# Moving the output stores of a multiply-and-GELU kernel to the ScalarE queue, in four pieces, each issued when its columns are done

## The chip, the cores and the metric

One core of a Trainium2 chip runs the kernel. The metric is the device time in microseconds (us), reported as the median of several runs. All runs quoted here were classed as fast (none is over 1.5% above the fastest run of its kernel), the profiled ones at a granted TensorE clock of 1.0, which is full speed. The span of a profile runs from the first instruction to the last and is some 1.3 us shorter than the reported time.

## The reference

```python
x, y: 1024 x 4096 float32
z = x * y
out = 0.5 * z * (1 + tanh(sqrt(2 / pi) * (z + 0.044715 * z ** 3)))
```

Two arrays of 16.78 MB are read and one is written. There is one multiply (VectorE) and one GELU (ScalarE) for each element.

## The kernel before

The arrays are seen as 128 partitions by 32768 columns. All of x has its own place in SBUF (the core's on-chip memory), where the product and the GELU are written too. Of y only 16384 columns fit at a time, so its second half is loaded in two quarters, each when the multiplies have freed its place. Everything that moves data is issued from SyncE, in this order: x first half, y first half, x second half, y third quarter, y last quarter, store of the first half, store of the second half.

```python
X_LOADS = [(0, 16384), (16384, 32768)]
Y_LOADS = [(0, 16384, 0), (16384, 24576, 0), (24576, 32768, 8192)]
STEP = 4096
STORES = [(0, 16384), (16384, 32768)]
...
    load_x(1)
    for i in (1, 2):
        nc.sync.wait_ge(sem_mul, (Y_LOADS[i][1] - Y_LOADS[1][0]) // STEP)
        load_y(i)
...
        nc.vector.wait_ge(sem_y[i], 16)
        for c in range(a, b, STEP):
            nc.vector.tensor_mul(...).then_inc(sem_mul, 1)
            n += 1
            nc.scalar.wait_ge(sem_mul, n)
            nc.scalar.activation(..., func=GELU).then_inc(sem_act, 1)

    for i, (a, b) in enumerate(STORES):
        nc.sync.wait_ge(sem_act, b // STEP)
        nc.sync.dma_start(out=out_r[:, a:b], in_=xs[:, a:b]).then_inc(sem_o[i], 16)
```

## Time and profile before

| before | |
|---|---|
| time | 120.78 us (120.68 to 120.92) |
| span of the profile | 119.5 us |
| DMA engines busy | 98.5% of the span |
| VectorE, ScalarE busy | 29%, 25% |
| last load lands | 80.79 us |
| last GELU ends | 93.30 us |

In the profile, "DMA" is the mean of the core's 16 DMA engines; its row cuts the span into 40 slices and gives tenths of busy time. "L87 DVE" is the multiply and "L94 ACT" the GELU. "SPq" and "ACTq" are issues of transfers on SyncE's and ScalarE's queues: one takes about 0.34 us and says nothing of how long the data move. (A line marked x2 spans from the start of its first issue to the end of its last.) The time of the data is in "to landing", the time from the issue to the last byte's completion. The lines themselves stand in the prediction below.

### The profile page before, as it was taken

The numbers are of one execution on the slowest core, as the hardware profiler recorded it, in microseconds if no ns is written. First come the engines' busy times: TensorE is split into PE (matmuls) and PEld (weight loads), VectorE is DVE, ScalarE is ACT, GpSimd is POOL, SyncE is SP. The second block draws the span as 40 slices with busy tenths as digits, with TensorE's granted clock in tenths as the row PEclk, the third lists the DMA queues.
The fourth block names the chain that finished last, engine by engine and source line by source line (L and its number), as shares of the span: only waits on it lengthen the run. The fifth ranks groups of instructions, "written<-read, shape, count | busy, mean of one in ns | idle before, by whom it ended". The sixth has DMA issues, their size and how long they took to land.

```text
span 119.5 us, 68 instructions
## 1 busy us (share of the span) xinstructions
DVE 35.0 (29%) x8; ACT 30.2 (25%) x9; POOL 0.2 (0%) x4
## 2 busy tenths in 40 slices
DVE  0000000000000199999600049959990000000000
ACT  3000000000000006797780000977479200000000
POOL 0000000000000000000000000000000000000000
DMA  9889888998899889988898989998899888988890
GB/s 351 351 373 680 351 351 351 636 417 351 351 636 417 351 351 526 526 351 351 351 526 351 504 373 482 395 526 351 351 395 658 351 351 351 702 351 351 351 680 22
DMA packets 1008, 50.33 MB, mean 421 GB/s; under 512 B 112, under 2 KB 112, under 8 KB 112
## 3 DMA queue, kind: packets, MB, share of 16 engines
q1 hardware_dynamic: 1008, 50.33, 98.5%
HBM read 33.55 MB, written 16.78 MB: 421 GB/s over the span
## 4 chain that ended last, share of the span: by engine, by line
DMA 53%; DVE 22%; ACT 3%; SPq 0%; issue 0%; DVEq 0%
DMA ys<-in_y_dram 53%; DVE xs L87 22%; ACT xs L94 3%; SPq L66 0%; DVEq L85 0%
## 5 line engine op out<-in xcount | busy, mean ns | idle before, releaser
L87 DVE TENSOR_TENSOR xs<-xs,ys 128x4096 f32<-128x4096 f32 x8 | 35.0, 4421 | 54.7 <-DMA ys<-in_y_dram 54.7
L94 ACT ACTIVATE xs<-xs 128x4096 f32<-128x4096 f32 x8 | 28.9, 3617 | 61.1 <-DVE xs L87 61.1
L94 ACT ACT_TABLE_LOAD x1 | 1.3, 1283 | 1.9 <-PEq L54 1.9
L120 POOL MEMSET const-bfloat16-1.0<- 128x1 bf16 x1 | 0.1, 102 | 0.0
L120 POOL MEMSET const-uint8-127<- 128x1 uint8 x1 | 0.1, 102 | 0.0
L120 POOL MEMSET const-float32-1.0<- 128x1 f32 x1 | 0.1, 99 | 0.0
L120 POOL MEMSET const-float32-0.0<- 128x1 f32 x1 | 0.1, 98 | 0.2 <-issue 0.2
## 6 DMA issues: line engine op xcount, KB each, us to landing
ys<-in_y_dram SPq DMA_DIRECT2D x2, 4096.0 KB, 21.1
xs<-in_x_dram SPq DMA_DIRECT2D x2, 40.3
out_dram<-xs SPq DMA_DIRECT2D x2, 31.9
ys<-in_y_dram SPq DMA_DIRECT2D x1, 40.8
```

The source lines that it names most:

```text
L87: nc.vector.tensor_mul(out=xs[:, c : c + STEP], in0=xs[:, c : c + STEP], in1=ys[:, r + c - a : r + c - a + STEP],).then_inc(sem_mul, 1)
L94: nc.scalar.activation(out=xs[:, c : c + STEP], in_=xs[:, c : c + STEP], func=GELU).then_inc(sem_act, 1)
L120: nc = _bacc.Bacc("TRN2", target_bir_lowering=False, num_devices=1)
```

## The change

The intent is to send out results as soon as they exist, on a queue of their own, so that they need not stand behind all loads.

```diff
-STORES = [(0, 16384), (16384, 32768)]
+STORES = [(0, 8192), (8192, 16384), (16384, 24576), (24576, 32768)]
...
             ).then_inc(sem_act, 1)
+            for k, (sa, sb) in enumerate(STORES):
+                if sb == c + STEP:
+                    nc.scalar.wait_ge(sem_act, n)
+                    nc.scalar.dma_start(
+                        out=out_r[:, sa:sb], in_=xs[:, sa:sb]
+                    ).then_inc(sem_o[k], 16)
 
-    for i, (a, b) in enumerate(STORES):
-        nc.sync.wait_ge(sem_act, b // STEP)
-        nc.sync.dma_start(out=out_r[:, a:b], in_=xs[:, a:b]).then_inc(sem_o[i], 16)
```

The text calls the four stores A to D, as the prediction does.

## The prediction

> **What bounds the kernel now.** I began with the page: its table of slices and its queue table say whether the engines that compute or the transfers set the time.
>
> ```profile
> span 119.5 us, 68 instructions
> DVE 35.0 (29%) x8; ACT 30.2 (25%) x9; POOL 0.2 (0%) x4
> ...
> DVE  0000000000000199999600049959990000000000
> ACT  3000000000000006797780000977479200000000
> ...
> DMA  9889888998899889988898989998899888988890
> ...
> q1 hardware_dynamic: 1008, 50.33, 98.5%
> ```
>
> VectorE and ScalarE stand idle for two thirds of the span. The 16 DMA engines are busy in every slice to the end, 98.5% of the span in all, on one queue. Every byte moved is needed (two inputs and one output of 16.78 MB), so the kernel is bound by transfers with hardly a gap, and the change removes no byte. It can only close or open gaps.
>
> The next view is the chain that ended last, in order of time, to see when each load lands, then the order of all instructions, to see when each store could go.
>
> ```profile
> 0.44 40.80 DMA ys<-in_y_dram
> ...
> 58.80 21.99 DMA ys<-in_y_dram
> ...
> 80.88 8.77 DVE xs L87 x2
> ...
> 89.68 3.62 ACT xs L94
> ```
>
> ```profile
> 50.13 3.62 ACT L94 ACTIVATE xs<-xs 128x4096 f32<-128x4096 f32 x1 [0.72 <-DVE xs L87]
> ...
> 58.80 3.62 ACT L94 ACTIVATE xs<-xs 128x4096 f32<-128x4096 f32 x1 [0.72 <-DVE xs L87]
> 62.45 31.22 SPq L100 DMA_DIRECT2D out_dram<-xs  x2
> ```
>
> The last load (y of the last 8192 columns) lands at 58.80 + 21.99 = 80.79 us; two multiplies and one GELU later, at 93.30, everything is computed. This last 12.5 us of arithmetic costs nothing, because the first store, 8.39 MB, was issued at 62.45 and stands in the same queue right behind the loads. The view of the store line shows how long it stood there:
>
> ```profile
> L100 SPq DMA_DIRECT2D out_dram<-xs x2: 343/346/348, 62.4 to 93.3; - x2
> ...
> DMA to landing us min/median/max: 26.1/31.9/37.7
> ```
>
> It lands at 62.45 + 37.7 = 100.1, that is 19.4 us after the last load: the 17.6 us before that it only waited its turn. The second store is issued at 93.3, before the first has ended, and lands at 93.3 + 26.1 = 119.4. So **the first store is a stock of 19.4 us of transfers that is kept back until the loads are over and covers the 12.5 us of arithmetic behind the last load.** That is what I look at in the change.
>
> The unit of a transfer is in the trace's records of single packets: one row of 64 KB takes 2.418 us on its engine and one of 32 KB 1.213 us, loads and stores alike; each engine carries 8 of the 128 rows. 16 x 65536 B / 2.418 us is 434 GB/s. So a transfer of 16384 columns takes 8 x 2.418 = 19.3 us and one of 8192 columns 8 x 1.213 = 9.7 us.
>
> **What the Trainium skill says.** (1) "DMA: Bandwidth & Descriptors", section "Where 436 GB/s comes from", gives 435 GB/s as the ceiling of the 16 engines; the 434 GB/s above agrees, so no faster rate is to be had from a second queue. (2) The same page, "Issuing engines are not separate DMA queues": transfers issued from ScalarE and SyncE run on the same 16 engines and interleave, and a second issuer saves only issue time. The kernel before has one queue, so its trace can't show this. (3) The same page, "Queues, rings and completion order": each engine goes round-robin between the queues that have work, a packet at a time. This is the step my number rests on most; again nothing in the trace before shows it, and the trace after will. (4) "Perfetto Trace Analysis", section "DMA Optimizations", recommends one issuing engine for inputs and another for outputs, and smaller chunks that start sooner, the latter where the DMA engines are generally idle. Here they are not: 98.5%.
>
> **The change part by part.** *Removed:* SyncE's two store issues and their waits for GELU; off the path until the end. *Added on ScalarE:* four waits for its own GELUs and four issues. An issue took 0.346 us on SyncE; I take the same, and 0.1 us (a guess) for the wait. ScalarE has 0.72 us of idle time before each GELU (the brackets above), so 0.45 us fits in, and the GELUs before the last pair are not late. *Moved:* where the stores lie among the loads. I name the four stores A to D and work through the time.
>
> The first packet of x moves 1.0 us after its issue starts in the packet records. A is ready at 50.13 + 3.62 = 53.75; with 0.1 for the wait and 1.0 to the first packet it moves from 54.8. B is ready at 62.42 and can move from 63.5. From 54.8 on both queues have work. The loads alone would have ended at 80.8. With equal turns, x's second half (5.8 us left, 2.4 packets of 64 KB) gives way to 2.4 packets of A: 2.9 us, landing near 63. Then come the 8 packets of y's third quarter against 8 of A and B: 9.7 + 9.7 = 19.4 us, landing at 82 to 83 in place of 70.3. Then y's last quarter: 8 packets against the 5.6 that A and B have left. By then all of A and B, 2 x 9.7 = 19.4 us, has gone ahead of the last load: 80.8 + 19.4 = 100.2. How turns are shared hardly matters to this sum, as long as the stores get about half.
>
> C is ready when y's third quarter, landed at 82.5, is through: two multiplies (8.76), a GELU (3.62) and 0.15 of waits, 95.0; it moves from 96, when some 2 to 3 packets of the last load are left, and takes 1 or 2 turns, 1.2 to 2.4 us. I worked through the turns of one engine packet by packet with these durations: the last load lands at 101.5, A and B are done by 95.5, C by 108.8. That working lands the old loads at 79.7, 1.1 us before their 80.8, because the records show a few packets of 1.8 to 3.2 us and some skew between engines; I take half of it as carried over: 102.0.
>
> Then the end, with nothing left to cover it: 102.0 + 0.1 (start) + 8.76 (two multiplies) + 3.62 (GELU) = 114.5. Meanwhile C has ended near 109.3 and the engines stand idle. D: 0.1 for the wait, 1.0 to the first packet, 8 x 1.213 = 9.7, and 0.3 from the last packet to the landing (records: 119.07 against 119.4): 11.1 us. The sum is 125.6 us of span. The profiled run before was reported at 120.85 us for a span of 119.5, so 1.35 more: **about 126.9 us**. As a check by gaps: the engines stand idle from 109.3 to about 115.6, 6.3 us, and 120.8 + 6.3 = 127.1. The gain of D being half as long as the old second store is nothing, since only the total and the gaps count.
>
> **The rivals.** *Loads keep precedence* (the stores get few turns while loads are queued): then A and B wait as before, the last load lands near 81, A to D drain behind it without a gap, and the time is 120.5 to 121. For it: the loads were issued long before. Against it: the skill's round-robin. A half-way share would land the last load early and leave some stock, 121 to 125. *Traffic in both directions at once moves more than 434 GB/s*: if a load and a store overlapped fully, the last load would land near 82, computing ends at 94.5 and D lands at 105.6, about 107 us. Against it: a load and a store cost the same 2.418 us a packet in the records and the skill has one ceiling for the engines. *Mixing costs rate*[...]: 3% over the some 45 us of mixing would add 1.3 us, for 128.3. No mixed stretch exists in the trace before, so I can't size it. *ScalarE becomes the bound* because its queue also issues: 25% busy, 0.72 us of slack a turn; if each issue took 1 us it would add 0.7 us at the end only.
>
> **Range and chances.** The fair-share sum gives 125 to 128 with the packet at which C comes in, the skew and the issue cost varied; the mixing loss would stretch it to 129, an uneven share would pull it down. I say 126.7, and 124.2 to 128.6 for eight times in ten. Slower by over 2% means above 123.2: 0.86, the fair share with any of its sizes. Within 2% needs load precedence or nearly: 0.10. Faster needs overlap of both directions: 0.04.
>
> **What would show the steps right or wrong.** Right: the wait of VectorE before y's third quarter grows from 11.7 to some 24 us and the last load lands near 102; the stores from ScalarE's queue land 20 us or more after issue for A and B and some 11 for D; the DMA row has a gap of 5 to 7 us near 109 to 115 and is full again to the end; the chain that ended last now ends with a store of about 11 us behind GELU; multiplies still take 4.42 and GELUs 3.62 us. Wrong: a last load at 81 (precedence), more than 440 GB/s while both queues are busy (overlap), packets longer than the shares explain (mixing loss), or GELUs that start late behind an issue (ScalarE).

## The result, and the profile after

The changed kernel takes **126.7 us** (126.5 to 126.73), against 120.81 us for the kernel before in the same rounds. The ratio is 1.0484, with a 95% interval of 1.0466 to 1.0502. A ratio is the mean time of one kernel's fast runs over that of the other's of the same rounds, so it is not quite the ratio of the medians. The change makes the kernel 4.8% slower.

The page of the changed kernel, its head, its table of slices and its queues:

```profile
span 125.4 us, 71 instructions
...
DVE 35.0 (28%) x8; ACT 30.2 (24%) x9; POOL 0.2 (0%) x4
...
DVE  0000000000000799997000000039940059920000
ACT  3000000000000037977900000000976001974000
...
DMA  9799799789779979999699999999999999703977
...
q1 hardware_dynamic: 720, 33.55, 63.1%
q10 hardware_dynamic: 576, 16.78, 31.0%
```

VectorE is busy for the same 35.0 us and ScalarE for the same 30.2. What is new is the second queue, q10, and a hole in the DMA row in the slices just before the last four, while VectorE and ScalarE work by themselves. In the packet records no engine moves anything from 109.72 to 115.00 us: **5.28 us**. The span grew by 5.9. The packets of both queues together took 118.0 us of an engine's time, against 117.7 before, so 0.3 us more is busy time, and the rest of the growth is idle.

The chain that ended last, in order of time (start, us, what):

```profile
0.42 40.92 DMA ys<-in_y_dram
...
58.90 42.72 DMA ys<-in_y_dram
...
101.71 8.77 DVE xs L87 x2
...
110.51 3.62 ACT xs L94
```

The last load is issued at 58.90, as before, but lands after 42.72 us and not after 21.99: at 101.62 instead of 80.79. The two multiplies and the GELU behind it take as long as ever. The order of instructions shows what went ahead of it:

```profile
53.88 0.38 ACTq L100 DMA_DIRECT2D out_dram<-xs  x1
...
62.55 0.34 ACTq L100 DMA_DIRECT2D out_dram<-xs  x1
83.55 8.76 DVE L87 TENSOR_TENSOR xs<-xs,ys 128x4096 f32<-128x4096 f32 x2 [24.68 <-DMA ys<-in_y_dram]
...
95.99 0.34 ACTq L100 DMA_DIRECT2D out_dram<-xs  x1
...
114.15 0.34 ACTq L100 DMA_DIRECT2D out_dram<-xs  x1
```

These are the four stores. A and B are issued 48 and 39 us before the last load lands, and are gone by then: B's last packet ends at 97.1. VectorE's wait for y's third quarter (in brackets) has grown from 11.70 to 24.68 us. The view of the store line gives the landings:

```profile
L100 ACTq DMA_DIRECT2D out_dram<-xs x4: 338/339/375, 53.9 to 114.2; - x4
...
DMA to landing us min/median/max: 11.1/19.7/36.1
```

D, issued last, needs 11.1 us to land and has the engines to itself. Finally the windows view of two stretches (VectorE, ScalarE and POOL busy, clock, DMA share, GB/s):

```profile
64.00:95.00 31.00, 8.76 (x2) 6.27 (x2) 0.00 (x0) 1.00 1.01 436
110.00:115.00 5.00, 0.47 (x1) 3.62 (x1) 0.00 (x0) 1.00 0.02 7
```

While loads and stores take turns, the engines carry 436 GB/s, as much as one queue of loads alone (435 in the first 41 us of the kernel before; the ends of such a window cut packets, so a few per cent are not to be read). The packet records are sharper: every one of the 395 rows of 32 KB that lie wholly within 64 to 95 us, 195 of loads and 200 of stores, took 1.213 us, the median of such a row on one queue. In the five microseconds before D the engines carry next to nothing.

### The profile page after: what moved, and what is told of

It reads as the page before. It is cut to its first block, busy times and chain, and to the rows that moved or that the text cites. A ratio compares the mean times of both kernels' runs of the same rounds, so it can differ in the third digit from the quotient of the medians.

```text
span 125.4 us, 71 instructions
## 1 busy us (share of the span) xinstructions
DVE 35.0 (28%) x8; ACT 30.2 (24%) x9; POOL 0.2 (0%) x4
## 4 chain that ended last, share of the span: by engine, by line
DMA 67%; DVE 21%; ACT 3%; SPq 0%; issue 0%; DVEq 0%
DMA ys<-in_y_dram 67%; DVE xs L87 21%; ACT xs L94 3%; SPq L66 0%; DVEq L85 0%
```

## The experiments

My theory: A and B were a stock of transfers that covered the arithmetic behind the last load, and the change spends it too early. The rivals are that ScalarE's queue costs something by itself, that smaller stores do, or that loads and stores in the same stretch slow each other. The first four kernels take the change apart, and of the last four, e7 is a half dose and the others try to bring the time back by other ways than undoing it. All gave correct results. For a whole view first (the hole is the time in which the packet records show no data packet on any engine; "before" took 120.95 us in both groups of runs, and 120.81 in the rounds of the change; landing and hole are of the one profiled execution, which in e2 was its slowest, 135.76 us):

| kernel | last load lands | hole before the last store | time | ratio to before |
|---|---|---|---|---|
| before | 80.79 | none | 120.95 | 1 |
| split alone (e1) | 80.89 | none | 120.99 | 1.0005 |
| move alone (e2) | 101.05 | 13.67 | 135.14 | 1.1166 |
| change, A and B held (e3) | 86.63 | none | 121.42 | 1.0034 |
| one queue, A and B first (e4) | 100.60 | 3.96 | 125.49 | 1.0371 |
| change, pieces of 4096 (e5) | 91.73 | none | 121.15 | 1.0014 |
| change, pieces of 2048 (e6) | 86.19 | none | 121.34 | 1.0038 |
| change, B held (e7) | 96.51 | 0.43 | 121.74 | 1.0064 |
| change, finer last quarter (e8) | 101.41 | none | 121.06 | 1.0010 |
| the change | 101.62 | 5.28 | 126.70 | 1.0484 |

In every row the time is that of before in the same rounds, plus the hole, plus 0.0 to 0.6 us.

### e1: the split alone

```diff
 # the kernel before, with
-STORES = [(0, 16384), (16384, 32768)]
+STORES = [(0, 8192), (8192, 16384), (16384, 24576), (24576, 32768)]
```

> The split alone: four stores of 8192 columns, all on SyncE's queue behind the loads, as in the kernel before. Theory (the stock of early stores is spent before the last load, so the arithmetic after it is bare): here nothing goes ahead of the last load, it lands at 80.8 us as before, and the time is that of before, 120.5 to 121.3. Rival (stores of 8192 columns, that is rows of 32 KB and twice as many packets, cost by themselves): 123 or more.

It took 120.99 us, ratio 1.0005 (0.9987 to 1.0023). The last load in the chain lands at 80.89:

```profile
58.61 22.28 DMA ys<-in_y_dram
```

Four stores with rows of 32 KB cost nothing against two with rows of 64 KB. That rival falls.

### e2: the move alone

```diff
 # the changed kernel, with
-STORES = [(0, 8192), (8192, 16384), (16384, 24576), (24576, 32768)]
+STORES = [(0, 16384), (16384, 32768)]
```

> The move alone: the two stores of 16384 columns go on ScalarE's queue as soon as their columns are done, without the split. Theory: the first store, 64 KB packets taking turns with 32 KB load packets, is all gone before the last load lands near 99 to 101; then 12.5 us of arithmetic with no transfer at all, then a store of 19.4 us: 133 to 136, worse than the change as a whole. Rival (the second queue or the issue on ScalarE costs a fixed amount per store): two issues instead of four, so 124 or less.

It took 135.14 us, ratio 1.1166 (1.1144 to 1.1189), by far the slowest, with half as many issues on ScalarE as the change. So no fixed cost per store can be the cause. Its DMA row shows the whole of the last arithmetic bare:

```profile
DMA  9997979979789797799998999899940000979777
```

The hole is 13.67 us long. The split, which costs nothing in e1, is thus worth 8.4 us once the stores go early: in the change, C is still there to cover part of the arithmetic.

### e3: the change with A and B held until y's third quarter has landed

```diff
 # the changed kernel, with (shortened: the kernel keeps 0 and 1 in a tuple)
+            if n == 5:
+                nc.scalar.wait_ge(sem_y[1], 16)
+                for k in (0, 1):
+                    store(k, 4)   # the wait on sem_act and the issue, as in the change
             nc.scalar.wait_ge(sem_mul, n)
...
-                if sb == c + STEP:
+                if sb == c + STEP and k not in (0, 1):
```

> The changed kernel, but ScalarE holds its first two stores until y's third quarter has landed (70.3 us), so that they share with the last load only. Queue, split, issues and mixing stay. Theory: the last load lands at 88 to 92 in place of 101.6, the second store and the third are the stock behind it, no gap, and the time is that of before, 120.5 to 121.5. Rivals (ScalarE's queue, the size of stores, loss by mixing loads and stores): 123.5 to 127.

It took 121.42 us, ratio 1.0034 (1.001 to 1.0058). ScalarE still issues all four stores, and A still takes turns with a load. The instructions in order of time, A and B issued together, the last quarter's multiplies, and the DMA row:

```profile
70.16 0.86 ACTq L84 DMA_DIRECT2D out_dram<-xs  x2
...
86.73 8.76 DVE L95 TENSOR_TENSOR xs<-xs,ys 128x4096 f32<-128x4096 f32 x2 [7.74 <-DMA ys<-in_y_dram]
```

```profile
DMA  9899888988898889888989997989898999999994
```

Issued 16 us later than in the change, A delays the last load by 5.8 us, where A and B delayed it by 20.8, and the transfers run on without a hole. Nearly all of the loss is a matter of when A and B go. Some 0.3% may remain. One step of the expectation missed: the last load landed at 86.63 and not at 88 to 92, because A's first packet came only 4.85 us after its issue (75.01). e7 meets this lateness again.

### e4: one queue, with A and B ahead of the last load

```diff
 # the kernel before with four stores, issued on SyncE in this order
     for i in (1, 2):
+        if i == 2:
+            store(0)
+            store(1)
         nc.sync.wait_ge(sem_mul, (Y_LOADS[i][1] - Y_LOADS[1][0]) // STEP)
         load_y(i)
...
+    store(2)
+    store(3)
```

> One queue only (SyncE's), four stores, but the first two are issued ahead of the last load, so there is no turn-taking and no store on ScalarE. Theory: the last load lands at 99 to 101 because both stores go ahead of it, the third store covers 9.7 us of the 12.5 us of arithmetic, a gap of 4 to 5 us opens before the last store, and the time is 124 to 125.5, most of the loss without ScalarE's queue. Rivals (ScalarE's queue, mixing): no loss, 121.

It took 125.49 us, ratio 1.0371 (1.0347 to 1.0395). Nothing is issued on ScalarE and nothing takes turns, and 4.5 of the change's 5.9 us are lost all the same. The last load in the chain, and the DMA row:

```profile
62.88 37.72 DMA ys<-in_y_dram
```

```profile
DMA  9798799779879977987899898999989899903977
```

It lands at 100.60, behind A and B. The hole of 3.96 us stands where the change has its own. The order in which transfers pass the engines makes the loss; the second queue is one way to get that order.

### e5 and e6: stores in smaller pieces

```diff
 # the changed kernel, with PIECE = 4096 (e5) or 2048 (e6)
-                    nc.scalar.dma_start(
-                        out=out_r[:, sa:sb], in_=xs[:, sa:sb]
-                    ).then_inc(sem_o[k], 16)
+                    for p in range(sa, sb, PIECE):
+                        nc.scalar.dma_start(
+                            out=out_r[:, p : p + PIECE], in_=xs[:, p : p + PIECE]
+                        ).then_inc(sem_o[k], 16)
```

The wait at the end is for the sum of the pieces. Queue, moment of the first issue and bytes are those of the change.

> The changed kernel with every store of 8192 columns issued as two of 4096 columns at the same moment, so store packets are 16 KB against load packets of 64 and 32 KB. If each engine takes turns by packets, the stores get one third and the last load lands near 91, early enough that stores are left to cover the arithmetic: 120.8 to 121.8. If turns are by bytes, or several packets of one queue go in one turn, the last load lands near 101 as in the changed kernel and the time is 126 to 127. Each extra issue costs ScalarE about 0.34 us, which it may not have before the next GELU: up to 0.3 us late, to no effect.

> As the one before with pieces of 2048 columns, 8 KB packets. Turns by packets: the stores get a fifth, the last load lands near 86, time 120.8 to 122. Turns by bytes: 126 to 127. The time from the last packet of a load to its landing, 1.5 us in the changed kernel and 0.3 to 0.4 before, should shrink to 0.6 or so if the landing's own record has to wait out one store packet.

They took 121.15 us (ratio 1.0014, 0.9997 to 1.0031) and 121.34 us (1.0038, 1.0016 to 1.006). The last load in the chain of e5, then of e6:

```profile
58.79 32.94 DMA ys<-in_y_dram
```

```profile
58.65 27.54 DMA ys<-in_y_dram
```

It lands at 91.73 and 86.19, in place of 101.62. Turns are therefore taken by packets, one row each, and not by bytes. The records do not name their engine, but joining those whose start meets another's end shows it: load rows of 32 KB (1.21 us) alternate one for one with store rows of 32 KB (1.21 us) in the change, of 16 KB (0.61 us) in e5 and of 8 KB (0.31 us) in e6. The counts agree: e5 has 192 rows of loads and 178 of stores wholly within 64 to 86 us, e6 176 and 192 within 64 to 82. A smaller row is a smaller share, and enough stores stay back to fill the hole. The expectation for ScalarE was low in e6: four issues took 2.04 us and delayed the next GELU by 1.4 us, which cost nothing there.

The expected sign of the completion came too. A load's last data packet is followed by a record of 4 bytes, which I take to raise its semaphore. From the end of the last load's last packet to the end of the last such record takes 1.21 us in the change, 0.61 in e5, 0.31 in e6: each time one store row. (The landing in the chain comes some 0.35 us after that record, so the expected 0.6 for e6 is 86.19 less 85.52, 0.67.)

### e7: the change with B held, a half dose

```diff
 # as e3 (shortened in the same way), but
-                for k in (0, 1):
+                for k in (1,):
...
-                if sb == c + STEP and k not in (0, 1):
+                if sb == c + STEP and k not in (1,):
```

> The changed kernel with only the second store held until y's third quarter has landed; the first goes as early as in the change. A half dose. Theory: y's third quarter lands near 80, the last load near 97 to 98, a gap of some 3 us is left before the last store, and the time is 122.5 to 124.5, between before and changed. If ScalarE's queue by itself costs: 126.7 unchanged.

It took 121.74 us, ratio 1.0064 (1.0047 to 1.0081): between before and the change, but **under the expected range**. The direction is right and the size is not. B is issued at 80.77, and I had its first packet 1.0 us later, as in the prediction. The records have it at 84.72, 3.95 us after its issue. By then the last load had sent 4 of its 8 packets on each engine without giving way, and it lands at 96.51, not at 97 to 98; D is issued at 109.04, and C's last packet ends at 109.46, so only 0.43 us stay uncovered.

```profile
58.72 37.79 DMA ys<-in_y_dram
```

Looking back, the same lateness is in the other kernels with two queues: A's first packet comes 4.1 us after its issue in the change (53.88 to 57.98), the first store's 4.2 us in e2 (62.34 to 66.51), and A's 4.85 us in e3; C in the change needed 3.3 us (95.99 to 99.28; B's last packet had ended at 97.12). On idle engines, D's comes after 0.85 us (114.15 to 115.00). In e3, as in e7, 64 rows of the last load, four for each engine, had started before the store's first. Why an engine sends so much of the older queue first is open; that it has rows already under way is only a guess.

### e8: the change with a finer last quarter

```diff
 # the changed kernel, with D cut in two and the last quarter in half steps
-STORES = [(0, 8192), (8192, 16384), (16384, 24576), (24576, 32768)]
+STORES = [
+    (0, 8192), (8192, 16384), (16384, 24576), (24576, 28672), (28672, 32768)
+]
...
-        for c in range(a, b, STEP):
+        step = STEP if i < 2 else STEP // 2
+        for c in range(a, b, step):
```

> The changed kernel with its last quarter computed in steps of 2048 columns and its last store cut into two of 4096 columns; all early stores stay as early. Theory: the last load still lands at 101.6, the first half of the last store is ready some 6.5 us later, when the third store is just ending, and the gap falls from 5.3 us to under 1 us: 120.8 to 122. If the loss lies in mixing or in ScalarE's queue and not in the bare tail: 126 to 127.

It took 121.06 us, ratio 1.001 (0.9995 to 1.0025). The last load in the chain, the last steps' first store, and the DMA row:

```profile
58.86 42.55 DMA ys<-in_y_dram
```

```profile
107.97 0.34 ACTq L103 DMA_DIRECT2D out_dram<-xs  x1
```

```profile
DMA  9899889988899889989969999999989898989996
```

The last load lands at 101.41, as late as in the change. All that the change does to queues, turns and early stores is there. Only D's first half is ready at 107.97 and not at 114.15, before C's last packet ends at 109.52, and the loss is gone. This is the strongest test: unless the finer steps gain something of their own, whatever else the change costs is not more than some 0.25%. I changed the steps and the cut of D together, so their shares are not told apart.

No version beat the kernel before. The best are level with it, because without a hole all of them take the 118 us of packets and a start and an end.

## Why the prediction was right

The time on record was 126.7 us, and 126.7 was measured. The mechanism was right; that the tenth fits is luck. The working gave 126.9 and, by gaps, 127.1, the number was set a little below both, and errors in the steps cancelled. The steps, one by one:

- **The bound and the ceiling** held. Rows of 1.213 us throughout the mixed stretch, one after another, rule out both rivals on rate, the faster one (both directions at once) and the slower one (a loss by mixing).
- **Round-robin by packets** held, shown by the alternation in the records and by e5 and e6. That a turn is one row was the prediction's own reading of the skill's "packet" (see the last section). Load precedence, the rival for an unchanged time, did not occur, except that a new store on busy engines waited 3.3 to 4.85 us for its first turn.
- **Nothing fixed on ScalarE**: an issue took 0.339 us in the middle against the assumed 0.346. The wait for its own GELU, guessed at 0.1 us, was 0.02 (110.51 + 3.62 to 114.15). The GELUs stayed on their beat.
- **A's entry** was wrong by 3 us: 54.8 predicted, 57.98 measured. It made no difference, because the sum only needs A and B to be through before the last load, and they were. In e7 the same error shows in the time.
- **The last load**: 102.0 predicted, 101.62 measured, by two errors that nearly cancel. C was to move from 96 and to take one or two turns (1.2 to 2.4 us) ahead of the last load's data. It took none: its first row starts at 99.28, after the last load's last row has started on every engine (98.82). And the working left out the completion that waits one store row, C's (1.21 us). How much of the 0.5 us taken in for skew between engines was real is not told apart.
- **The hole** was predicted as 109.3 to 115.6, 6.3 us, and measured as 109.72 to 115.00, 5.28, so the check by gaps had it 1.0 us too long. It took the time to be that of before plus the hole; measured, 0.6 us come on top. D needed the predicted 11.1 us from its issue to its landing.
- **The sum**: 125.6 us of span against 125.4.
- **One sign was not seen**: the chain that ended last was to end with a store of 11 us. The view ends with the GELU and shows no store, neither before nor after; D's 11.1 us stand in the view of the store line.

The expected gain of the change, sending results out sooner, was never to be had. Before, the first store waited 17.6 us in the queue, and that wait was not idle time of the engines. It was what kept them supplied when the arithmetic had nothing to give. e1, e4 and e8 together show that the loss is this hole and little else. What is left beyond the holes, up to 0.6 us (in the change, e2 and e4), is not explained, except that the packets take somewhat longer in sum: 118.0 us of an engine's time in the change and 118.6 in e6, in place of 117.7.

## What to carry to other kernels

When the transfers are busy all the time, sending something earlier only moves something else later, so ask what the moved transfer was covering: transfers that wait for nothing are worth keeping for the stretch in which the last load's arithmetic has yet to produce anything. A second queue is a change of order: on shared engines it gave each queue one row a turn, so the length of its rows set its share. If stores must go early, cut the work behind the last load fine enough that its first piece is ready before the older stores run out.

## What the Trainium skill lacked or had wrong

- "DMA: Bandwidth & Descriptors", section "Queues, rings and completion order": it says that an engine drains a whole packet, typically 9 to 17 descriptors (orders to move one piece each), before it turns to another queue. Its round-robin by packets is confirmed here, but a turn was one row of 8, 16, 32 or 64 KB. It lacks the consequence that a queue's share goes by its row size: the last load landed at 101.62, 91.73 and 86.19 us with store rows of 32, 16 and 8 KB. It also gives no size for how long a load's completion is held up by another queue: it came 1.21, 0.61 and 0.31 us after the last data, one store row each time.
- The same page, "Latency and other measured facts", gives about 600 ns for the first byte. On idle engines the first packet came 0.85 us after the start of an issue of 0.34 us, so 0.51 us after its end, which is near it; on engines busy for another queue it came after 3.3 to 4.85 us, and no page was found that has this.
- The same page, "Issuing engines are not separate DMA queues", says that issuing from several engines only saves issue time. It lacks that the order of transfers, which changes too, can cost time: the move alone cost 11.7% (e2).
- "Perfetto Trace Analysis", section "DMA Optimizations", says that separate issuing engines for inputs and outputs may make sense, above all with loops, and names no case against it. Here, with the DMA engines 98.5% busy and the stores issued as soon as they were ready, it cost 4.8%; with A and B held back on the same queue, 0.3% (e3).
- No page was found to state the rate of loads and stores mixed on two queues. Here a row of 32 KB took 1.213 us in both directions while they took turns, as in loads alone (436 and 435 GB/s in the windows).
